# Layer 1's attention on ScalarE, VectorE and GpSimd: an order written by queues and slots in place of the scheduler's

## The chip, the core and the metric

The kernel runs on one core of one Trainium2 chip. The metric is the device time of one execution in microseconds (us). A core has five engines with instruction queues of their own: TensorE (PE, matmuls; PEld is its weight load), VectorE (DVE), ScalarE (ACT), GpSimd (POOL) and SyncE (SP, which issues the DMAs). An engine takes its instructions in the order in which they stand in its queue; an instruction that waits holds up all that stand behind it.

## What is computed

The reference is an encoder of two layers over 1024 tokens of width 1024, in fp32. Layer 0 mixes tokens with a neighbourhood attention, layer 1 with a dense differential attention of 8 heads; both end with a gated convolutional feed-forward part and a gated embedding. The change is in layer 1's attention:

```python
def diff_attention(h, w_qkv, lam, subln_g, w_o, t5_table, lambda_init):
    q, k, v = jnp.split(h @ w_qkv, 3, axis=-1)      # q, k: 8 heads x 2 maps of 64; v: 8 heads of 128
    ...
    def block_fn(args):                             # one block of 128 queries
        bias = t5_table[t5_bucket(kpos[None, :] - qpos[:, None])]
        s = jnp.einsum('bhmqd,bhmkd->bhmqk', qb, k).astype(jnp.float32) + bias[None, :, None]
        a = jax.nn.softmax(s, axis=-1)
        w = a[:, :, 0] - lam_full * a[:, :, 1]
        return jnp.einsum('bhqk,bhkd->bhqd', w.astype(v.dtype), v)
    o = lax.map(block_fn, (q_blocks, jnp.arange(nb)))
    ...
    o = rms_norm(o, subln_g) * (1.0 - lambda_init)
    return o @ w_o
```

## The kernel before

For fp32 accuracy on TensorE, each operand of a large matmul is split into a high part (ACT rounds it, `high`, L231) and a low part (DVE subtracts, `low`, L234); with a scale they are L241 and L242. One product of two such operands is three matmuls (L268, L269, L270).

Layer 1's attention (`da`) goes through 64 chunks: 8 heads by 8 blocks of 128 queries. The loop over n is software-pipelined and written in the order that PE follows word for word: `da_values(n-1)` (16 matmuls, L971), `da_scores(n+1)` (12 matmuls, L928), the first `da_turn(n)` (four transposes of the weights E, L955, which ACT copies into wT, L958), some of the stream, the second turn (copied at L960), some of the stream, `da_out(n-1)` (a transpose of the normed row os, L988, copied by ACT into ot at L996), and again the stream. Beside PE a chunk has on DVE: ss (L975), os (L980), two biased scores with their minimum (L750), then c, the sums' reciprocals (L938 to L940) and the weights E (L941); on POOL the root of ss (L280); on ACT the square (L974), the two exponentials (L754), wT twice, and ot.

The stream, `da_stream`, is a generator that makes the projections q, k and v and hands PE three matmuls for each unit; `tick` draws 6.3 units a chunk for the first 16 chunks and 5.3 after. The first two heads are projected plainly (`keys`, `queries`, `values`). All others come in nine `Pair`s, each two blocks of weights done by seven products instead of eight:

```python
PRODUCTS = (
    ("A11", "B11", 0), ("S2", "T2", 1), ("A12", "B21", 0), ("S3", "T3", 1), ("S1", "T1", 2), ("A22", "T4", 1), ("S4", "B22", 2),
)
```

Each names a weight operand (A or a sum S), an activation operand (B or a sum T) and one of three accumulators, which lie in two banks of PSUM by turns. So a product brings: a weight split (ws, ACT then DVE), S sums on POOL (L116 to L119), and an evacuation of a bank in `put`: p1 (ACT, L164), u (DVE, L166), c11 (ACT, L169, in v pairs), w (DVE, L173), c5 (ACT, L175), p2 (DVE, L181), u2 (DVE, L184), and w plus c5 on POOL (L178). For kq pairs the outputs are split into the head's q and k (L231 to L242); for v pairs PE turns them (L299, copied by ACT at L625; the plain ones from raw, L634). The T sums, 36 adds on POOL (L576 to L586), are made once at the start, split, sent to DRAM (L562) and loaded again for each pair (L595). Near the end the stream makes splits of the layer's input embeddings (L1892).

On PE the order is written out by hand; on ACT, DVE and POOL the tile framework's scheduler sets it, from a simulated timeline, with a few hints: `behind` and `job` put an instruction of the stream behind one of the attention, and `hurry` runs what is in a list of postponed splits, `jobs`.

Of the kernel before, what the change touches and what calls it, by code (L numbers as in the profile page):

```python
# [16 lines left out]
P = 128  # L17
# [81 lines left out]
class Pair:  # L99


    def __init__(self, trunk, W, room, kind, j):
        self.trunk, self.room, self.kind, self.j = trunk, room, kind, j
        self.src = (W[KT + j], W[j]) if kind == "kq" else (W[2 * KT + j], W[2 * KT + j + 1])
        self.A, self.o, self.ps, self.made, self.w = {}, {}, {}, [], 0
    def load(self, n):
        k = self.trunk
        w = k.page(k.raw, "raw", (P, KT, P))
        k.nc.sync.dma_start(w, self.src[n])
        self.A[f"A{n + 1}1"], self.A[f"A{n + 1}2"] = w[:, :4], w[:, 4:]  # L110

    def sums(self):
        A, tt = self.A, self.trunk.nc.gpsimd.tensor_tensor
        S = lambda n: self.room[:, n].rearrange("p (k n) -> p k n", k=4)
        A["S1"], A["S2"], A["S3"], A["S4"] = (S(n) for n in range(4))
        tt(out=A["S1"], in0=A["A21"], in1=A["A22"], op=ALU.add)  # L116
        tt(out=A["S2"], in0=A["S1"], in1=A["A11"], op=ALU.subtract)
        tt(out=A["S3"], in0=A["A11"], in1=A["A21"], op=ALU.subtract)
        tt(out=A["S4"], in0=A["A12"], in1=A["S2"], op=ALU.subtract)  # L119

    def operand(self, q):
        k, trunk = PRODUCTS[q][0], self.trunk

        def do():
            self.o[k] = trunk.operand(self.A[k])
            return trunk.did

        trunk.jobs.append(do)
# [8 lines left out]
    def bank(self, n, q):  # L137
        first = n not in self.ps
        if first:
            self.ps[n] = self.trunk.bank(self.trunk.pj)  # L140
        return self.ps[n], first

    def out(self, row, half, src, turns, turn, wait):

        k, j = self.trunk, self.j
        if self.kind == "v":
            turns.append([wait, turn(self.h[row], half, src, 2 * (j + row) + half)])
            return
        s = slice(half * 512, half * 512 + 512)
        if row:  # L150
            k.split(src, self.h[:, 0, s], self.h[:, 1, s], -0.125)
        else:
            k.split(src, self.h[:, 2, s], self.h[:, 3, s])
        self.made.append(src)
        if len(self.made) == 4:
            k.qk[j] = self.h

    def put(self, a, turns, turn):

        nc, ps = self.trunk.nc, self.ps  # L160
        tt, act = nc.vector.tensor_tensor, nc.scalar.activation
        c11, p1, u, w, c5 = (self.room[:, n] for n in (1, 4, 5, 6, 7))
        if a == "A11":
            act(p1, ps[0], AF.Copy)  # L164
        elif a == "S2":
            tt(out=u, in0=ps[1], in1=p1, op=ALU.add)  # L166
        elif a == "A12":
            if self.kind == "v":
                act(c11, ps[0], AF.Copy)  # L169
            self.out(0, 0, c11 if self.kind == "v" else ps[0], turns, turn, 2)  # L170
        elif a in ("S3", "S1"):
            if a == "S3":
                tt(out=w, in0=ps[1], in1=p1, op=ALU.add)  # L173
            else:
                act(c5, ps[2], AF.Copy)  # L175
            self.w += 1
            if self.w == 2:
                nc.gpsimd.tensor_tensor(out=w, in0=w, in1=c5, op=ALU.add)  # L178
                self.out(1, 1, w, turns, turn, 4)
        elif a == "A22":  # L180
            tt(out=p1, in0=ps[1], in1=p1, op=ALU.add)  # L181
            self.out(1, 0, p1, turns, turn, 3)
        else:
            tt(out=u, in0=ps[2], in1=u, op=ALU.add)  # L184
            self.out(0, 1, u, turns, turn, 3)


class Trunk:
# [328 lines left out]

    def da_stream(self, hT, x, first, mid):
# [4 lines left out]
        turns = []  # L523
        self.third = True

        def step():
            for t in turns:
                t[0] -= 1
            if self.open and turns and turns[0][0] < 0:
                turns.pop(0)[1]()  # L530
# [3 lines left out]
        def plain(w, tb, wait=None):  # L534
            s = slice(tb * 512, tb * 512 + 512)
            ps = self.bank(self.pj)
# [11 lines left out]
        tt, pool = nc.vector.tensor_tensor, nc.gpsimd.tensor_tensor  # L548
# [9 lines left out]
        made = []  # L558

        def put(m, key, t):  # L560
            did = self.split(t, ring[:, m % 4, 0], ring[:, m % 4, 1])
            nc.sync.dma_start(stash[key][m // 3], raw[:, m % 4])  # L562
            return did

        def sums(n):

            k = n // 2
            self.all_jobs()
            if made:
                self.jobs += [lambda a=a: put(*a) for a in made.pop()]  # L570
            if n == 8:
                return
            b = [tuple(f(a)[:, k] for a in x) for x in (B11, B12, B21, B22)]
            t1, t2, t3, t4 = room[:, k], room[:, 4 + 3 * (k % 2)], room[:, 5], room[:, 6]
            if n % 2 == 0:
                pool(out=t1, in0=b[1][0], in1=b[0][0], op=sub)  # L576
                pool(out=t1, in0=t1, in1=b[1][1], op=add)
                pool(out=t1, in0=t1, in1=b[0][1], op=sub)
                pool(out=t2, in0=b[3][0], in1=t1, op=sub)
                pool(out=t2, in0=t2, in1=b[3][1], op=add)  # L580
                made.append([(3 * k, "T2", t2)])
# [1524 lines left out]
```

## Time and profile before

| | |
|---|---|
| median of 3 executions | 2718.63 us (2714.75 to 2719.02) |
| profiled execution | 2721.1 us |
| its span | 2719.3 us (36972 instructions) |
| PE busy | 2665.1 us, 98% |
| DVE busy | 1970.9 us, 72% |
| ACT busy | 1373.0 us, 50% |
| POOL busy | 561.5 us, 21% |

The profile is one execution, taken by the hardware profiler. The profiled execution's own time is 1.8 us above its span. A row of the timeline reads: start us, duration us, engine, line, operation, output from inputs, form, count, and in brackets the idle time just before with what ended it. The layer-1 attention lies between about 1300 and 1910 us of the span.

### The profile page before, as it was taken

The page shows a single profiled execution, that of the slowest core. Times are in us where ns is not written, and L with a number is a line of the kernel's source. Part 1 is how long each engine was busy: PE and PEld are TensorE (multiplying, and loading weights), DVE is VectorE, ACT ScalarE, POOL GpSimd, SP SyncE. Part 2 cuts the span into 40 slices and gives each one's busy share as a digit, 9 for nine tenths or more (in the row PEclk, how much of TensorE's full clock was granted, in tenths as well). Part 3 has the DMA queues.
Part 4 walks back from the last instruction along what each step waited for, and adds up shares of the span by engine and source line. Part 5 has one row for each costly group of instructions (what it writes and reads, how often), then busy time and mean ns, then how long its engine had stood idle before and what let it go on. Part 6 is the DMA issues. An engine that isn't in the chain of part 4 may idle for free.

```text
span 2719.3 us, 36972 instructions
## 1 busy us (share of the span) xinstructions
PE 2665.1 (98%) x13384; PEld 2197.9 (81%) x13384; DVE 1970.9 (72%) x3379; ACT 1373.0 (50%) x2595; POOL 561.5 (21%) x526
## 2 busy tenths in 40 slices
PE   8999999999999999999999999999999999999999
PEld 6888887878888888888777877777878888878887
DVE  5777776699777777676667767776699777768674
ACT  5555556454444444554456666665454444444452
POOL 2221220003433300000722222210103334300000
PEclk9999999999999999999999999999999999999999
DMA  6223226424232373333345655552423333374342
GB/s 182 85 66 105 75 93 200 132 68 137 92 116 96 122 271 124 113 128 119 119 144 198 201 170 194 176 176 84 159 71 130 103 109 100 112 249 139 116 136 101
DMA packets 149785, 360.91 MB, mean 133 GB/s; under 512 B 14009, under 2 KB 40889, under 8 KB 149602
## 3 DMA queue, kind: packets, MB, share of 16 engines
q1 hardware_dynamic: 149602, 358.55, 40.3%
q8 instruction: 105, 1.72, 0.3%
q14 instruction: 78, 0.64, 0.1%
HBM read 277.79 MB, written 92.90 MB: 136 GB/s over the span
## 4 chain that ended last, share of the span: by engine, by line
PE 82%; DVE 7%; ACT 5%; issue 2%; POOL 2%; DMA 1%; SPq 0%; ACTq 0%; DVEq 0%; POOLq 0%
PE b L268 19%; PE b L269 19%; PE b L270 19%; PE g L1135 6%; PE m L1135 5%; PE b L971 3%; ACT E L754 2%; PE s L928 2%; PE b L299 2%; PE b L1135 2%; PE av L821 2%; PE b L955 1%; PE b L794 1%; DVE E L750 1%; DVE r L234 1%
## 5 line engine op out<-in xcount | busy, mean ns | idle before, releaser
L268 PE MATMUL b<-r,ws 128*128 128x512 f32 (+1 forms) x1308 | 533.2, 408 | 1.7 <-DVE r L403 1.7
L269 PE MATMUL b<-r,ws 128*128 128x512 f32 (+1 forms) x1308 | 506.3, 387 | 0.6 <-DVE r L234 0.5
L270 PE MATMUL b<-r,ws 128*128 128x512 f32 (+1 forms) x1308 | 506.7, 387 | 0.0
L754 ACT ACTIVATE E<-E,mn 128x1024 f32<-128x1024 f32 (+2 forms) x256 | 221.5, 866 | 148.3 <-DVE mn L750 148.1
L270 PEld LDWEIGHTS b<-r,ws 128*128 128x128 f32 x1308 | 246.8, 189 | 51.8
L268 PEld LDWEIGHTS b<-r,ws 128*128 128x128 f32 x1308 | 247.8, 189 | 47.6 <-issue 3.3
L269 PEld LDWEIGHTS b<-r,ws 128*128 128x128 f32 x1308 | 248.3, 190 | 35.6 <-DVE r L234 1.9
L268 PE MATMUL b<-r,wa 128*128 128x512 f32 x688 | 268.1, 390 | 1.9 <-DVE B L1527 1.9
L270 PE MATMUL b<-r,wa 128*128 128x512 f32 x688 | 267.9, 389 | 0.0
L269 PE MATMUL b<-r,wa 128*128 128x512 f32 x688 | 267.7, 389 | 0.0
L280 POOL TENSOR_TENSOR ss<-ss,mhalf 128x1 f32<-128x1 f32 x128 | 83.6, 654 | 857.7 <-DVE ss L276 382.1
L268 PE MATMUL b<-r,r 128*128 128x512 f32 x648 | 254.4, 393 | 1.3 <-DVE facc L1731 0.7
L269 PE MATMUL b<-r,r 128*128 128x512 f32 x648 | 252.8, 390 | 1.9 <-DVE r L234 1.9
L270 PE MATMUL b<-r,r 128*128 128x512 f32 x648 | 252.5, 390 | 0.0
L231 ACT ACTIVATE r<-raw 128x512 fp32r<-128x512 f32 (+1 forms) x168 | 108.7, 655 | 195.4 <-PE b L269 169.9
L234 DVE TENSOR_TENSOR ws<-raw,ws 128x512 fp32r<-128x512 f32 (+3 forms) x177 | 170.8, 971 | 49.6 <-ACT ws L231 48.0
L231 ACT ACTIVATE ws<-raw 128x512 fp32r<-128x512 f32 (+3 forms) x177 | 122.3, 697 | 109.0 <-PE b L270 52.0
L234 DVE TENSOR_TENSOR r<-raw,r 128x512 fp32r<-128x512 f32 (+1 forms) x168 | 124.8, 749 | 70.3 <-ACT r L231 67.3
L1135 PE MATMUL m<-r,ws 128*128 128x512 f32 x672 | 157.3, 392 | 0.0
L1135 PE MATMUL g<-r,ws 128*128 128x512 f32 x672 | 155.8, 391 | 0.0
L268 PEld LDWEIGHTS b<-r,wa 128*128 128x128 f32 x688 | 129.1, 188 | 29.9 <-DVE B L1527 3.2
L750 DVE CUSTOM_DVE_ANT_0 E<-s,T 128x1024 f32<-128x1024 f32 x128 | 151.1, 1216 | 1.0 <-PE s L928 0.9
(227 smaller groups left out, 5344.9 us busy)
## 6 DMA issues: line engine op xcount, KB each, us to landing
r<-stashT SPq DMA_DIRECT2D x108, 512.0 KB, 4.5
raw<-in_w_in SPq DMA_DIRECT2D x86, 512.0 KB, 3.5
raw<-in_qkv SPq DMA_DIRECT2D x48, 512.0 KB, 3.9
spillS<-r SPq DMA_DIRECT2D x88, 256.0 KB, 2.7
r<-in_ffn_w_out SPq DMA_DIRECT2D x40, 512.0 KB, 6.6
raw<-spillS SPq DMA_DIRECT2D x40, 512.0 KB, 3.6
spillA<-B SPq DMA_DIRECT2D x66, 256.0 KB, 2.7
raw<-spillA SPq DMA_DIRECT2D x30, 512.0 KB, 3.9
```

What stands on the lines that cost most here:

```text
L231: return self.nc.scalar.activation(hi, src, AF.Copy).ins
L234: return self.nc.vector.tensor_tensor(out=lo, in0=src, in1=hi.bitcast(F32), op=ALU.subtract).ins
L268: mm(out, sta[0], mov[0], start=first, stop=False, skip_group_check=onto)
L269: mm(out, sta[0], mov[1], start=False, stop=False, skip_group_check=onto)
L270: mm(out, sta[1], mov[0], start=False, stop=last, skip_group_check=onto)
L280: self.nc.gpsimd.tensor_tensor(out=ss, in0=ss, in1=self.mhalf, op=ALU.pow)
L299: self.nc.tensor.transpose(t[:, k * P : k * P + P], h[:, c : c + P], self.ident)
L750: nc.vector.tensor_tensor_reduce(out=e, in0=s, in1=bias, scale=1.0, scalar=3e38, op0=ALU.add, op1=ALU.min, accum_out=mn)
L754: self.exp = nc.scalar.activation(e, e, AF.Exp, bias=mn, scale=-1.0, accum_out=sm).ins
L821: nc.tensor.matmul(out, V[:, kb, m], a[:, at : at + w].rearrange("p k t -> p (k t)"), start=g % 2 == 0 and i + z == 0, stop=g % 2 == 1 and ...
L971: nc.tensor.matmul(o, wT[:, k], V[:, k], start=k == 0, stop=k == KT - 1)
L1135: mm(out[half], a, b[:, w], start=first and k + z == 0, stop=last and k == n - 1 and z == 2)
```

## The change

The attention of layer 1 gets a region in which ACT, DVE and POOL follow the program's order as PE does; it begins before `da_scores(0)` and ends at the last product:

```python
+            self.region = self.tc.manual_schedule(engines={ENG.Activation, ENG.DVE, ENG.Pool})
+            self.region.__enter__()
...
+            if last and q == 6:
+                self.flush()
+                self.third = False
+                self.region.__exit__(None, None, None)
```

What a product needs besides PE is no longer issued at once. Each split, sum and evacuation goes into a queue ("A" for ACT, "D" for DVE, "G" for POOL) with a modelled cost, a key, the keys that must come first, and a modelled date from which it is ready. `slot` takes from such a queue as long as room is left, evacuations first (`hot`) and weight splits after other things; `force` takes what PE is about to need, with what must come first:

```python
+    def later(self, eng, do, cost, key=None, first=(), ready=None):
+        self.queue[eng].append((do, cost, key, first, self.now if ready is None else ready))
+    def slot(self, eng, room, at, urgent=False):
+        q, end = self.queue[eng], at + room
+        self.now = at
+        while end - at > 0.3:
+            can = [
+                n for n, (_, _, _, first, ready) in enumerate(q)
+                if ready <= at and all(k in self.did_keys and self.ready_at.get(k, 0) <= at for k in first)
+            ]
+            hot = [n for n in can if q[n][2] and self.hot & set(q[n][2])]
+            if not (hot if urgent else can):
+                return
+            cold = [n for n in can if not (q[n][2] and q[n][2][0] == "a")]
+            at += self.pop(eng, (hot or cold or can)[0], at)
+    def force(self, *keys):
+        for key in keys:
+            while key not in self.did_keys:
+                ...
+                self.pop(eng, n)
```

The places in a chunk are fixed, by a modelled clock of 8.6 us for each chunk:

```python
             for n in range(N + 1):
+                self.now = self.base = 8.6 * n + self.extra
...                                               # da_values: behind the root, ahead of os
+            self.slot("A", 1.3, at + 2.5), self.slot("D", 0.7, at + 2.7), self.slot("G", 4.3, at + 3.3)
...
                     self.da_turn(x, n, 0)
+                if n + 1 < N:
+                    self.da_exp(n + 1, 0)
+                self.now = self.base + 3.9
                 self.tick(0.34)
                 if n < N:
                     self.da_turn(x, n, 1)
+                if n + 1 < N:
+                    if self.third:
+                        self.slot("A", 0.7, self.base + 6.7, True)
+                    self.da_exp(n + 1, 1)
+                    if self.third:
+                        self.slot("D", 1.6, self.base + 6.4)
+                    self.da_weights(n + 1)
...
                     self.da_out(x, n - 1, oT)
+                if self.third:
+                    self.slot("G", 2.8, self.base + 7.8), self.slot("A", 1.9, self.base + 8.4), self.slot("D", 1.2, self.base + 10.1)
```

For this the softmax is cut in three: `biased` (both biased scores in `da_scores`), `da_exp` and `da_weights`. Smaller parts: the T sums are planned for units 10, 17, 24, ... 59 instead of 10, 18, 27, ... 76; a pair's second load and its S sums come one product earlier (at products 2 and 4 instead of 3 and 5); kq pairs copy c11 out on ACT too, as v pairs did, instead of splitting it from the bank (six more ACT copies); turns of v wait until their source is ready by the model; a head's q and k are handed over when its splits are asked for; the embeddings' first two loads come together and their splits go through the queues:

```python
-        plan = {u: lambda n=n: sums(n) for n, u in enumerate((10, 18, 27, 36, 45, 53, 61, 68, 76))}
-        plan |= {58: lambda: pairs[0].load(0), 70: lambda: pairs[0].load(1), 80: first_operands, 83: first_sums}
+        plan = {u: lambda n=n: sums(n) for n, u in enumerate((10, 17, 24, 31, 38, 45, 52, 59))}
+        plan |= {60: lambda: pairs[0].load(0), 70: lambda: pairs[0].load(1), 76: late_stash, 80: first_operands, 83: first_sums}
...
-            if self.kind == "v":
-                act(c11, ps[0], AF.Copy)
-            self.out(0, 0, c11 if self.kind == "v" else ps[0], turns, turn, 2)
+            k.later("A", lambda: act(c11, ps[0], AF.Copy), 0.6, key("c11"), mine("S2"))
+            self.out(0, 0, c11, turn)
+            k.holds(ps[0], key("c11"))
...
-            if after and q == 3:
-                self.all_jobs()
+            if after and q == 2:
                 after.load(1)
-            if after and q == 5:
-                self.all_jobs()
+            if after and q == 4:
                 after.sums()
```

PE's and SP's instructions stay the same in number; a few turns of v and the embeddings' units shift by some units of the stream. What moves on ACT and DVE is shown at three places. Names: E the (biased, then exponentiated) scores, mn and sum their minimum and sum, b a bank of PSUM, r pages of split operands or of the products' room, ws split weights.

ACT at the start of the attention, before: the exponentials of chunk 0 (L754), with the table load, then a T split, a copy of v (L634), a weight split, two T splits and the first wT copy.

```order
L241 ACTIVATE r_1548_11126<-b_1559_11238 128x512
L754 ACT_TABLE_LOAD
L754 ACTIVATE E_1566_11292,sum_11296<-E_1566_11292,mn_11294 128x1024
L754 ACTIVATE E_1567_11293,sum_11300<-E_1567_11293,mn_11298 128x1024
L231 ACTIVATE r_1549_11127<-r_1550_11128 128x512
L634 ACTIVATE raw_11270<-b_1562_11271 128x512
L231 ACTIVATE ws_11339<-raw_11337 128x1024
L231 ACTIVATE r_1549_11127<-r_1550_11128 128x512 x2
L958 ACTIVATE wT_11401<-b_1587_11402 128x512
```

The same place now (L249 is the high part, L598 a scaled or plain high part of q or k, L1110 the exponential, L1136 the wT copy):

```order
L249 ACTIVATE r_1549_11127<-r_1550_11128 128x512
L598 ACTIVATE r_1548_11126<-b_1560_11239 128x512
L249 ACTIVATE r_1549_11127<-r_1550_11128 128x512 x3
L772 ACTIVATE raw_11281<-b_1563_11282 128x512
L249 ACTIVATE ws_11342<-raw_11237 128x1024
L1110 ACT_TABLE_LOAD
L1110 ACTIVATE E_1567_11313,sum_11319<-E_1567_11313,mn_11315 128x1024
L1110 ACTIVATE E_1568_11314,sum_11320<-E_1568_11314,mn_11317 128x1024
L1136 ACTIVATE wT_11391<-b_1586_11392 128x512
```

Four T splits, the copy of v and the weight split moved ahead of the table load and the first exponential.

ACT in chunk 28, before, from the square (L974) to ot (L996):

```order
L974 ACTIVATE os_14069,ss_14070<-b_2125_14060,sum_13929 128x128
L231 ACTIVATE ws_14074<-raw_13617 128x512
L958 ACTIVATE wT_14108<-b_2139_14109 128x512
L754 ACTIVATE E_2131_14092,sum_14096<-E_2131_14092,mn_14094 128x1024
L169 ACTIVATE r_1550_11128<-b_2088_13889 128x512
L960 ACTIVATE wT_14108<-b_2141_14125 128x512
L754 ACTIVATE E_2132_14093,sum_14100<-E_2132_14093,mn_14098 128x1024
L231 ACTIVATE ws_14131<-r_1550_11128 128x512
L996 ACTIVATE ot_14139<-b_2125_14060,subg 128x128
```

Now, from the square (L1150) to ot (L1172) and the split behind it:

```order
L1150 ACTIVATE os_14082,ss_14083<-b_2127_14073,sum_13936 128x128
L1136 ACTIVATE wT_14111<-b_2139_14112 128x512
L1110 ACTIVATE E_2132_14102,sum_14109<-E_2132_14102,mn_14104 128x1024
L1136 ACTIVATE wT_14111<-b_2140_14127 128x512
L184 ACTIVATE r_1550_11128<-b_2088_13891 128x512
L1110 ACTIVATE E_2133_14103,sum_14110<-E_2133_14103,mn_14106 128x1024
L1172 ACTIVATE ot_14145<-b_2127_14073,subg 128x128
L249 ACTIVATE ws_14148<-r_1550_11128 128x512
```

The copy of c11 out of bank b_2088 moved from between the first exponential and the second wT copy to behind that copy, and the weight split from ahead of the first wT copy away to behind ot.

DVE in chunk 41, before, from the first biased score (L750) to the weights (L941); L181 is p2, L242 a low part:

```order
L750 ISA E_2357_15176,mn_15178<-s_15162,T_11275 128x1024
L750 ISA mn_15178 128x1
L750 ISA E_2358_15177,mn_15182<-s_15163,T_11275 128x1024
L750 ISA mn_15182 128x1
L181 TENSOR_TENSOR r_1550_11128<-b_2311_14942,r_1550_11128 128x512
L938 RECIPROCAL c_15186<-sum_15184 128x1
L234 TENSOR_TENSOR ws_15219<-r_1550_11128,ws_15219 128x512
L939 SCALAR_TENSOR_TENSOR c_15186<-sum_15180,c_15186,neglam 128x1
L242 SCALAR_TENSOR_TENSOR r_2293_14869<-r_1550_11128,r_2293_14869 128x512
L940 RECIPROCAL sum_15180<-sum_15180 128x1
L941 SCALAR_TENSOR_TENSOR E_2357_15176<-E_2358_15177,c_15186,E_2357_15176 128x1024
```

Now, from behind the weights of the chunk before (L188 is p2, L252 a low part, L1151 ss, L1156 os, L1103 the biased scores) to the last reciprocal, behind which the weights L1120 stand:

```order
L188 TENSOR_TENSOR r_1550_11128<-b_2310_14940,r_1550_11128 128x512
L252 TENSOR_TENSOR ws_15143<-r_1550_11128,ws_15143 128x512
L1151 TENSOR_SCALAR ss_15168<-ss_15168 128x1
L252 TENSOR_TENSOR ws_15145<-raw_14938,ws_15145 128x512
L1156 TENSOR_SCALAR os_15167<-b_2352_15158,sum_15021,ss_15168 128x128
L1103 ISA E_2357_15190,mn_15192<-s_15176,T_11296 128x1024
L1103 ISA mn_15192 128x1
L1103 ISA E_2358_15191,mn_15194<-s_15177,T_11296 128x1024
L1103 ISA mn_15194 128x1
L1117 RECIPROCAL c_15222<-sum_15197 128x1
L1118 SCALAR_TENSOR_TENSOR c_15222<-sum_15196,c_15222,neglam 128x1
L1119 RECIPROCAL sum_15196<-sum_15196 128x1
```

p2 and a low part moved from between the biased scores and the weights to ahead of ss, and nothing stands between the reciprocals any more.

More of the change, by code (lines that the diff above doesn't have):

```diff
@@ L115, in sums @@
[L115 to L119, printed above, removed]
-    def operand(self, q):
[L122 to L128, printed above, removed]
+        A, k, prev = self.A, self.trunk, self.prev
@@ L130, in begin, with high @@
+    def operand(self, q):
+        a, k = PRODUCTS[q][0], self.trunk
+        def high():
+            o = self.o[a] = k.page(k.ws, "ws", (P, 2, 4, P), F32R)
+            k.high(self.A[a], o[:, 0])
+            k.later("D", lambda: k.low(self.A[a], o[:, 0], o[:, 1]), 0.75, self.key(a), ready=k.ends + 0.1)
+        k.later("A", high, 0.62, self.key(a + " high"), [self.key(a + " sum")] if a[0] == "S" else [], self.loaded)
     def begin(self, x):
@@ L516, in qkv_stream, with pop @@
             yield from self.second_out()
+    def later(self, eng, do, cost, key=None, first=(), ready=None):
+        self.queue[eng].append((do, cost, key, first, self.now if ready is None else ready))
+    def pop(self, eng, n=0, at=None):
+        do, cost, key, first, ready = self.queue[eng].pop(n)
+        self.force(*first)
+        self.ends = (self.now if at is None else at) + cost
+        if key is not None:
+            self.ready_at[key] = self.ends
+        do()
+        self.did_keys.add(key)
+        return cost
@@ new lines, in turn_now, with flush, split_later, high @@
+    def turn_now(self, key):
+        n = [t[2] for t in self.turns].index(key)
+        for t in self.turns[: n + 1]:
+            t[1]()
+        del self.turns[: n + 1]
+    def flush(self):
+        while any(self.queue.values()):
+            self.pop(next(e for e in "DAG" if self.queue[e]))
+    def split_later(self, src, hi, lo, scale=None, key=None, cost=(0.62, 0.75), first=(), ready=None):
+        nc = self.nc
+        def high():
+            if scale is None:
+                self.high(src, hi)
+            else:
+                nc.scalar.activation(hi, src, AF.Copy, scale=scale)
+            self.later("D", low, cost[1], key, ready=self.ends + 0.1)
+        def low():
+            if scale is None:
+                self.low(src, hi, lo)
+            else:
+                nc.vector.scalar_tensor_tensor(out=lo, in0=src, scalar=scale, in1=hi.bitcast(F32), op0=ALU.mult, op1=ALU.subtract)
+        self.later("A", high, cost[0], key and (*key, "high"), first, ready)
@@ L518, in da_stream, with take, holds @@
+    def take(self):
+        if len(self.banks) == 2:
+            self.force(*self.banks.pop(0)[1])
+        ps = self.bank(self.pj)
+        self.banks.append((ps, []))
+        return ps
+    def holds(self, ps, key):
+        next(b for b in self.banks if b[0] is ps)[1].append(key)
     def da_stream(self, hT, x, first, mid):
@@ L1866, in embeddings @@
         todo = [lambda n=n: job(n) for n in range(4)]
-        self.jobs += todo[:2]
+        if x is None:
+            self.jobs += todo[:2]
+        else:
+            begin(self.raw, "raw"), begin(self.raw, "raw")
+            for n in range(2):
+                self.split_later(raws[n], *a[n], None, ("a", n), (1.05, 1.25))
         self.after_values = [] if layer else todo[2:]
```

325 lines of the change are left out of this document (209 added, 116 removed).

## Prediction

> **What bounds the kernel now.** I read the page first: how busy the engines are and which of them carries the chain that ended last.
>
> ```profile
> span 2719.3 us, 36972 instructions
> PE 2665.1 (98%) x13384; PEld 2197.9 (81%) x13384; DVE 1970.9 (72%) x3379; ACT 1373.0 (50%) x2595; POOL 561.5 (21%) x526
> PE 82%; DVE 7%; ACT 5%; issue 2%; POOL 2%; DMA 1%; SPq 0%; ACTq 0%; DVEq 0%; POOLq 0%
> ```
>
> PE is 98% busy and carries 82% of the chain. The change leaves PE's instructions as they are, so it can win only PE's idle time and the time in which PE is throttled, and only where attention of layer 1 runs, 1310 to 1910 us. So the second view is the busy time of each engine in four stretches of it, and, for the clock, one short window (the columns are: window, its length, busy us of PE, PEld, DVE, ACT, POOL with their counts, granted clock, DMA share, GB/s).
>
> ```profile
> 1310.00:1340.00 30.00, 26.38 (x148) 20.25 (x144) 21.80 (x25) 14.62 (x25) 29.21 (x20) 1.00 0.30 107
> 1340.00:1400.00 60.00, 54.10 (x327) 43.41 (x328) 42.17 (x80) 34.82 (x73) 20.24 (x19) 0.97 0.37 130
> 1400.00:1800.00 400.00, 390.57 (x2483) 315.74 (x2482) 288.19 (x572) 250.86 (x528) 92.04 (x86) 1.00 0.57 192
> 1800.00:1910.00 110.00, 102.50 (x619) 83.20 (x618) 72.71 (x143) 65.10 (x135) 6.57 (x12) 0.97 0.29 98
> ...
> 1392.00:1394.00 2.00, 2.00 (x7) 1.51 (x6) 1.72 (x5) 1.44 (x5) 0.00 (x0) 0.50 0.97 347
> ```
>
> PE's idle time is 3.6, 5.9, 9.4 and 7.5 us, together 26.4 us. The clock of 0.97 in two stretches is a loss of its own: 3% of 60 us is 1.8 us and of 110 us 3.3 us, together 5.1 us. It falls to 0.50 behind a wait, as the last row shows. **At most 26.4 + 5.1 = 31.5 us, 1.2%, can be won.** Third, the waits of PE there (engine, line, what it waited for: total us, times, longest):
>
> ```profile
> PE b L988 <- DVE os L980: 8.2, 5, 3.5
> PE b L971 <- ACT wT L960: 4.0, 7, 1.0
> PE b L299 <- ACT wT L960: 2.5, 2, 1.7
> PE b L268 <- ACT ws L1892: 2.5, 2, 1.8
> PE b L299 <- ACT wT L958: 1.9, 1, 1.9
> PE b L955 <- DVE ss L975: 1.6, 2, 1.3
> PE b L299 <- ACT raw L634: 1.3, 1, 1.3
> ...
> PEld b L971 <- ACT wT L960: 8.9, 12, 1.4
> ```
>
> Nearly all name a softmax result that came late (os, wT), and the late ones have sums or splits in front of them. One steady chunk, last, for the durations:
>
> ```profile
> 1508.03 1.95 PE L971 MATMUL b<-v,wT 128*128 128x128 f32 x16
> 1511.35 0.68 DVE L234 TENSOR_TENSOR ws<-r,ws 128x512 fp32r<-128x512 f32 x1
> 1512.47 0.41 DVE L980 TENSOR_SCALAR os<-b,sum,ss 128x128 f32<-128x128 f32 x1 [0.44 <-POOL ss L280]
> 1512.80 1.21 DVE L750 CUSTOM_DVE_ANT_0 E<-s,T 128x1024 f32<-128x1024 f32 x1
> 1515.20 0.58 ACT L960 ACTIVATE wT<-b 128x512 f32<-128x512 f32 x1
> 1515.68 1.14 ACT L754 ACTIVATE E<-E,mn 128x1024 f32<-128x1024 f32 x1
> 1516.01 1.95 PE L971 MATMUL b<-v,wT 128*128 128x128 f32 x16
> 1517.48 1.27 DVE L941 SCALAR_TENSOR_TENSOR E<-E,c,E 128x1024 f32<-128x1024 f32 x1
> ```
>
> From values to values (L971) the chunk takes 1516.01 − 1508.03 = 7.98 us, and it waits nowhere. DVE and ACT are 72% and 63% busy between 1400 and 1800 (288.19 and 250.86 of 400): there is room in sum, so only order matters.
>
> **The gains.** (1) The longest os wait:
>
> ```profile
> 1383.46 2.99 DVE L234 TENSOR_TENSOR r<-r,r 128x512 fp32r<-128x512 f32 x3
> 1387.56 1.00 POOL L280 TENSOR_TENSOR ss<-ss,mhalf 128x1 f32<-128x1 f32 x1
> 1390.82 0.33 PE L988 MATMUL b<-ident,os 128*128 128x128 f32 x1 [3.50 <-DVE os L980]
> 1809.85 0.33 PE L988 MATMUL b<-ident,os 128*128 128x128 f32 x1 [2.60 <-DVE os L980]
> ```
>
> Three low parts stand on DVE ahead of ss, POOL takes the root late, and os falls behind both biases. With the written order os stands before the biases in every chunk, with at most one filler between ss and it. I count the 3.5 us as won, and 1.0 of the three short ones (8.2 − 3.5 − 2.6 = 2.1), and the half clock behind it: 1.8 us. The 2.6 us at 1809.85 stays: four splits of the embeddings stand there in the new order too. Sum 6.3.
>
> (2) The waits for the second wT copy, 4.0 + 2.5 us. Before, an evacuation could stand between the first exponential and that copy; the order now has 4 such fillers in the whole attention for 13. Won in proportion, 9/13 of 6.5 = 4.5. Of PEld's 8.9 us, 4.9 more than PE's own, I count a third, 1.5. The raw wait of 1.3 and the ss wait of 1.3 go too, since raw copies now wait for a modelled date and no split stands inside the weights chain (15 before, none now): 2.6. Sum 8.6.
>
> **The costs.** (3) The start of attention:
>
> ```profile
> 1313.32 2.54 POOL L579 TENSOR_TENSOR r<-r,r 128x512 f32<-128x512 f32 x2
> 1309.63 1.28 ACT L754 ACT_TABLE_LOAD   x1
> 1312.54 1.15 ACT L754 ACTIVATE E<-E,mn 128x1024 f32<-128x1024 f32 x1 [1.64 <-DVE mn L750]
> 1315.99 2.20 DVE L941 SCALAR_TENSOR_TENSOR E<-E,c,E 128x1024 f32<-128x1024 f32 x1
> 1318.15 1.05 ACT L231 ACTIVATE ws<-raw 128x1024 fp32r<-128x1024 f32 x1
> 1321.16 0.66 PE L955 MATMUL b<-ident,E 128*128 128x128 f32 x4
> 1324.56 0.63 ACT L231 ACTIVATE r<-r 128x512 fp32r<-128x512 f32 x1 [5.36 <-POOL r L584]
> 1326.96 0.66 PE L299 MATMUL b<-ident,raw 128*128 128x128 f32 x4 [1.93 <-ACT wT L958]
> ```
>
> ACT's queue is now written: four T splits, a raw copy, a weight split and the table load stand ahead of the first exponential, and the last of these splits needs POOL's 14th T sum. Before, the 14th ended at 1313.32 + 2.54 = 1315.86, when the exponentials were over. From there: two splits 1.26, raw copy 0.58 (as wT's), weight split 1.05, table 1.28, to 1320.0; two exponentials at 1.25 with their read-outs, to 1322.5; c and weights 3.2 as before (from 1312.54 + 2 × 1.25 = 1315.0 to the end of L941, 1318.19, with POOL adding beside them) or, with L941 at 1.27 and POOL idle, about 1.7: to 1324.2 or 1325.7. PE wanted the turn at 1321.16: it waits 3.0 to 4.5 us, I take 3.6, about the middle. It replaces the 1.9 at 1326.96, and I add 1.8 for half clock behind it, since the wait of 3.50 had it and the one of 1.93, where the granted clock stayed 1.00, had not. Net 3.6 − 1.9 + 1.8 = 3.5.
>
> [...]
>
> (4) Evacuations in fixed places. A copy from PE's bank that stood ahead of exponentials now stands behind the second wT copy or later; an ACT copy takes 0.58 us, and where PE's next product wants the bank in the same chunk (chunks 14, 20, 29, 41, 50) the product waits. In five chunks, 0.6 us each (one ACT copy): 3.0. No wait for a bank shows before; so the bounds are 0 (the copy has the other bank's product as cover) and 5 × 1.14 = 5.7 (an exponential ahead of each); a gain is excluded, because no wait is there to win. In a written order a filler that waits for its own input also holds up all that is queued behind it: on ACT the next exponential, on DVE the next bias, on POOL the next root. The fillers are dealt by a model of 8.6 us for each chunk, where this one takes 7.98, so an input can be up to 0.6 us later than dealt; I put that into the range, not into the sum.
>
> (5) Splits of the embeddings, 4 × 0.63 = 2.5 us, stand on ACT between the first exponential and the second wT copy of a chunk near the end: 1.0 (0 if the stream ahead of that chunk's values covers them, 2.5 if nothing does; I take a value nearer 0, because the fourth of a chunk's stream that follows the second turn lies there, some 0.16 × 8 = 1.3 us). First operand of the first pair, whose low now follows both biases: 0.5 (0 to 1.2). A u2 sum that now stands behind L941 while the last turn of the first v pair wants it: 1.0 (0 to 1.27). Sum 2.5.
>
> The six more c11 copies, 6 × 0.58 = 3.5 us on ACT, cost nothing while ACT is 63% busy; if that cover goes they cost 3.5. Pair loads issued one product earlier, on SP, and the T sums, planned closer together on POOL, cost nothing but what (3) has: no wait of PE names a load in this stretch, and POOL is 92.04 of 400 us busy after 1400.
>
> **Sum:** −6.3 − 8.6 + 3.5 + 3.0 + 2.5 = −5.9 us against the profiled execution, 2719.3 + 1.8 around the span = 2721.1, hence 2715. That execution lies 2.5 us above the median of the runs, 2718.63, so the forecast in the runs' terms is 2718.6 − 5.9 = 2712.7; of the 4.4 us of idle time that the quoted waits do not name (26.4 − 22.0) I count a third, 1.5, as won, thus **2711**. For no change I take ±0.2%, 5.4 us, about what a measurement of this kernel can tell: the gain is just above it, and the likeliest case's own range is 2703 to 2716.
>
> **The rivals.** (A) Slower: the place of evacuations becomes PE's wait. There are 63 products, each with one. Before, they went when ready. If each bank comes 0.3 us late in mean, the cost (4) is 63 × 0.3 = 19 us instead of 3: −14.9 + 3.5 + 2.5 + 19 = +10, 2729. It decides from (14.9 − 6.0 + 5.4)/63 = 0.23 us in mean, above which the kernel is slower by over 0.2%. For it: both biases are 2 × 1.21 us during which DVE takes nothing else, and an ACT copy can meet 1.14. Against: a product is 12 matmuls and banks are two, so most have a product's time to spare. Chance 0.22.
>
> (B) Nothing measurable: the gains are real, but the start costs 4.5 + 1.8, DVE's fillers between L941 and ss (71 now, 51 before) make new os waits of 0.7 us (one low part) in 10 chunks: −5.9 + 0.9 + 7 = +2.0, which is 2721, or with half of the new os waits 2718. Chance 0.22.
>
> (C) Nearly all waits go: of 31.5 us remain the 3.6 + 1.8 at the start and the embeddings' 2.6; 2718.6 − 31.5 + 8 = 2695. For it: DVE and ACT have room in sum, and a chunk without fillers in its way waits nowhere. Against: the start alone keeps 5.4. Chance 0.15.
>
> (D) POOL holds DVE. L941 took 1.27 us alone and 2.20 us beside POOL's sums at 1315.99, and POOL now has five T sums in a row (5 × 1.27 = 6.4 us) in each of four early chunks, so that a root behind them also waits: 4 to 6 chunks by 0.93 us is 5 us, and the result 2716. Against: the T sums end early in attention. Chance 0.08. [...]
>
> **How the numbers follow.** The own forecast has 0.33, A 0.22, B 0.22, C 0.15, D 0.08. Faster by over 0.2% is below 2713.2: all of C, 0.15, three quarters of the own forecast, 0.25, and a third to a half of B and D by their low ends, 0.12; together 0.52. Slower by over 0.2% is above 2724: nearly all of A, 0.20, and B's high end, 0.02. The rest, 0.26, is within. The range runs from C less 3 us (one embedding wait gone as well), 2692, to A, 2729; below it I leave 0.06 and above it, where banks come over 0.3 us late, 0.11.
>
> **What would show it.** (1) right if no wait for os of over 1.5 us is left near 1390, and the clock of 0.50 there is gone. (2) right if the waits for the second wT copy come to under 2 us. (3) right if PE's first turn of E waits 3 to 4.5 us for the weights. (4) shows as waits of L268 on the copies of p1, c11 and c5, or on u, p2; over 15 us of them is rival A. D shows as L941 at over 2 us. The idle time of PE from 1310 to 1910 should be near 21 us for 26.4, of which 8 in the first 30 us. The forecast would be wrong if PE's order hid a wait at products that no row of before has.

## The result, and the profile after

The changed kernel takes 2697.95 us (median of 4, 2696.8 to 2699.0) for 2716.69 us before (median of 4, 2714.09 to 2719.02): a ratio of 0.9931, 95% interval 0.9914 to 0.9948. It is faster by 0.7%, some 19 us, where 2711 was forecast: the sign and the range held, the likeliest case's own range, 2703 to 2716, did not. Its profiled execution took 2696.8 us. The two profiled executions lie 24.3 us apart (2721.1 and 2696.8), more than the medians, at mean granted clocks of 0.997 and 0.999; of 13 further executions of the kernel before, the three at 0.999 took 2715.6 to 2715.9 us and the six at 0.997 took 2717.4 to 2720.7.

The busy times by stretch show where the time came from (columns as in the prediction; the attention is the same work, though it ends some 23 us earlier here, so the last window reaches further into what follows):

```profile
span 2695.0 us, 36988 instructions
PE 85%; DVE 6%; ACT 3%; issue 2%; DMA 2%; POOL 1%; SPq 0%; DVEq 0%; ACTq 0%; POOLq 0%
...
1310.00:1340.00 30.00, 26.77 (x140) 21.58 (x141) 16.75 (x28) 15.08 (x26) 12.77 (x10) 0.94 0.34 123
1340.00:1400.00 60.00, 58.79 (x368) 47.56 (x368) 49.95 (x84) 38.20 (x82) 32.90 (x27) 1.00 0.40 139
1400.00:1800.00 400.00, 396.24 (x2536) 322.61 (x2533) 299.31 (x593) 263.12 (x550) 81.08 (x88) 1.00 0.57 195
1800.00:1910.00 110.00, 107.08 (x631) 87.36 (x630) 75.48 (x139) 62.56 (x131) 8.77 (x16) 1.00 0.36 118
```

PE is idle for 11.1 us of these 600, for 26.4 before. Of the half clock, 5.1 us before, 1.8 us (6% of 30) are left, all in the first window. The waits of PE in 1310 to 1910 us are now these, 10.4 us in all for 25.8 (L1133 is the turn of E, L286 to L288 the three matmuls of a product, L759 the copy of a turned v, L2092 the copy of the embeddings' products, L1892 before):

```profile
PE b L1133 <- DVE E L1120: 4.0, 2, 3.2
PE b L1164 <- DVE os L1156: 2.3, 2, 1.3
PE b L286 <- ACT ws L2092: 1.4, 2, 0.7
PE b L1147 <- ACT v L759: 0.8, 1, 0.8
PE b L1147 <- ACT wT L1136: 0.7, 1, 0.7
PE b L1331 <- ACT ws L2092: 0.5, 1, 0.5
PE b L286 <- DVE r L194: 0.5, 1, 0.5
PE b L288 <- DVE ws L252: 0.2, 1, 0.2
```

Read against the list of before: L1164 is the transpose of os, 2.3 us for 8.2; L1147 is values, and L317 (turns of v), which waited 5.7 us for wT and raw, is gone. 3.2 us of the first row are the start that term (3) of the prediction described. The rows of L286 for r and of L288 are all that the evacuations and operands in fixed places cost: 0.7 us. The embeddings' copies (ws L2092) cost 1.9 us for 4.1; of before, the list in the prediction has 2.5 of these, and this row the rest:

```profile
PE b L1135 <- ACT ws L1892: 1.6, 1, 1.6
```

### The profile page after: what moved, and what is told of

The parts are those of the page before. It is cut to its first block, busy times and chain, and to the rows that moved or that the text cites. A ratio compares the mean times of both kernels' runs of the same rounds, so it can differ in the third digit from the quotient of the medians.

```text
span 2695.0 us, 36988 instructions
## 1 busy us (share of the span) xinstructions
PE 2658.3 (99%) x13384; PEld 2195.6 (81%) x13384; DVE 1971.6 (73%) x3380; ACT 1377.5 (51%) x2600; POOL 547.9 (20%) x526
## 4 chain that ended last, share of the span: by engine, by line
PE 85%; DVE 6%; ACT 3%; issue 2%; DMA 2%; POOL 1%; SPq 0%; DVEq 0%; ACTq 0%; POOLq 0%
PE b L286 19%; PE b L287 19%; PE b L288 19%; PE g L1331 6%; PE m L1331 5%; PE b L1147 4%; PE s L1092 3%; PE b L1133 2%; PE b L317 2%; PE b L1331 2%; PE av L985 2%; PE b L958 1%; ACT E L1110 1%; DVE r L252 1%; DMA x<-in_x 1%
## 5 line engine op out<-in xcount | busy, mean ns | idle before, releaser
L286 PE MATMUL b<-r,ws 128*128 128x512 f32 (+1 forms) x1308 | 533.2, 408 | 2.4 <-DVE r L421 1.7
L288 PE MATMUL b<-r,ws 128*128 128x512 f32 (+1 forms) x1308 | 506.5, 387 | 0.2 <-DVE ws L252 0.2
L288 PEld LDWEIGHTS b<-r,ws 128*128 128x128 f32 x1308 | 246.4, 188 | 52.6 <-DVE ws L252 1.0
L286 PEld LDWEIGHTS b<-r,ws 128*128 128x128 f32 x1308 | 247.1, 189 | 50.7 <-issue 3.3
L298 POOL TENSOR_TENSOR ss<-ss,mhalf 128x1 f32<-128x1 f32 x128 | 76.0, 595 | 959.6 <-DVE ss L1151 430.6
L286 PE MATMUL b<-r,wa 128*128 128x512 f32 x688 | 268.0, 390 | 2.0 <-DVE B L1723 2.0
L288 PE MATMUL b<-r,wa 128*128 128x512 f32 x688 | 267.9, 389 | 0.0
L286 PE MATMUL b<-r,r 128*128 128x512 f32 x648 | 254.4, 393 | 1.2 <-DVE facc L1927 0.6
L288 PE MATMUL b<-r,r 128*128 128x512 f32 x648 | 252.4, 390 | 0.0
L249 ACT ACTIVATE r<-raw 128x512 fp32r<-128x512 f32 (+1 forms) x168 | 108.7, 655 | 194.3 <-PE b L287 169.1
L252 DVE TENSOR_TENSOR ws<-raw,ws 128x512 fp32r<-128x512 f32 (+3 forms) x177 | 171.2, 973 | 44.8 <-ACT ws L249 42.5
L249 ACT ACTIVATE ws<-raw 128x512 fp32r<-128x512 f32 (+3 forms) x177 | 122.4, 698 | 108.1 <-PE b L288 51.9
L252 DVE TENSOR_TENSOR r<-raw,r 128x512 fp32r<-128x512 f32 (+1 forms) x168 | 124.7, 748 | 71.2 <-ACT r L249 68.2
L1110 ACT ACTIVATE E<-E,mn 128x1024 f32<-128x1024 f32 x128 | 146.8, 1147 | 20.1 <-DVE mn L1103 18.1
L286 PEld LDWEIGHTS b<-r,wa 128*128 128x128 f32 x688 | 129.1, 188 | 29.9 <-DVE B L1723 3.3
L288 PEld LDWEIGHTS b<-r,wa 128*128 128x128 f32 x688 | 129.1, 188 | 27.9 <-DVE wa L252 1.1
```

Of the source, the lines that this page charges most:

```text
L249: return self.nc.scalar.activation(hi, src, AF.Copy).ins
L252: return self.nc.vector.tensor_tensor(out=lo, in0=src, in1=hi.bitcast(F32), op=ALU.subtract).ins
L286: mm(out, sta[0], mov[0], start=first, stop=False, skip_group_check=onto)
L288: mm(out, sta[1], mov[0], start=False, stop=last, skip_group_check=onto)
L298: self.nc.gpsimd.tensor_tensor(out=ss, in0=ss, in1=self.mhalf, op=ALU.pow)
L1110: self.exp = self.nc.scalar.activation(e, e, AF.Exp, bias=mn, scale=-1.0, accum_out=sm).ins
```

## The experiments

### Is it the order that gains, or what the program says?

Two kernels separate the two. The first keeps the new program and takes the written order away, by a region that names PE alone:

```diff
-            self.region = self.tc.manual_schedule(engines={ENG.Activation, ENG.DVE, ENG.Pool})
+            self.region = self.tc.manual_schedule(engines={ENG.PE})
```

> The changed kernel without its region: queues, slots, cut softmax, earlier T sums and the rest stay, but ACT, DVE and POOL are placed by the scheduler again. Theory T (the gain is the fixed order on ACT, DVE and POOL, which keeps fillers from between ss and os, and from ahead of the second wT copy): most of the gain of 18.7 us is lost, 2710 to 2720, and waits for os and wT are back at 8 us or more. Rival R1 (the program's new sequence and dates are enough, whoever places them): within 3 us of the changed kernel, 2695 to 2702.

Measured: 2718.02 us, ratio to before 1.0004 (0.9994 to 1.0013). All of the gain is gone, as theory T says. PE's waits in 1310 to 1910 us:

```profile
PE b L1164 <- DVE os L1156: 6.9, 6, 2.6
PE b L317 <- ACT wT L1136: 5.3, 5, 2.4
PE b L1147 <- ACT wT L1136: 4.2, 6, 1.5
PE b L1147 <- ACT v L759: 2.8, 2, 2.3
```

os waits 6.9 us for 8.2 before, wT 9.9 us (with a row of 0.4 that is not shown) for 8.4: the waits are back, that of os a little below the 8 us expected. The second puts the cut softmax into the kernel before (`da_exp` behind each turn, `da_weights` behind the second):

```diff
...
+                if n + 1 < N:
+                    self.da_exp(n + 1, 0)
                 self.tick(0.34)
...
+                if n + 1 < N:
+                    self.da_exp(n + 1, 1)
+                    self.da_weights(n + 1)
```

> The kernel before with one part of the change alone: the softmax cut in three, so that in the program each exponential follows a turn and the weights follow the second exponential; the scheduler places it. Theory T: no gain of more than 4 us, 2713 to 2720, since the scheduler sets the order anyway. Rival R1: half of the gain or more, 2708 or less.

Measured: 2716.42 us, ratio 0.9996 (0.9987 to 1.0005). Nothing, so R1 falls twice.

### Which engine's order?

Three kernels leave one engine each to the scheduler and keep the other two in the written order; only the set in `manual_schedule` differs.

> The changed kernel with ACT and POOL in the written order and DVE left to the scheduler. Theory D1 (os and the biases were late because of what stood on DVE): most of the gain goes, 2709 or more, with os waits of over 5 us. Rival D2 (ACT's order carries the gain): 2702 or less.

> The changed kernel with DVE and POOL in the written order and ACT left to the scheduler. Theory D1: 2698 to 2704, a few waits for wT come back. Rival D2: 2709 or more, with waits for wT of 8 us or more.

> The changed kernel with ACT and DVE in the written order and POOL left to the scheduler. Theory D3 (the root behind POOL's sums made the longest os wait, with the order of POOL alone): the os wait and half clock come back between 1380 and 1400 us, 2703 or more. Theories D1 and D2: POOL has room after 1400 us, 2697 to 2701.

| written order on | time, us | ratio to before | above the changed kernel |
|---|---|---|---|
| all three | 2697.95 | 0.9931 (0.9914 to 0.9948) | |
| ACT, POOL | 2705.31 | 0.9961 (0.9946 to 0.9976) | 7.4 |
| DVE, POOL | 2699.57 | 0.9940 (0.9924 to 0.9957) | 1.6 |
| ACT, DVE | 2711.16 | 0.9980 (0.9970 to 0.9989) | 13.2 |
| none | 2718.02 | 1.0004 (0.9994 to 1.0013) | 20.1 |

POOL, the engine that is busy least, costs most when its order is left out. Not all of its 13.2 us is lost in steady chunks: at the start ACT waits longer for POOL's sums (7.5 us at a time for 4.7), PE waits 4.9 us for the first turn instead of 3.2, and the half clock lasts 6.8 us instead of 3.4, from 1322.8 us, still in the wait, to 1329.6 by windows of 1 us (clock 0.57 over 1322 to 1330; PE works in 4.3 us of it, so 2.1 us are lost for 1.7). DVE's share lies between D1's and D2's numbers, without the long os waits that D1 expected (1.5 us in all). D1's number for ACT (2698 to 2704) held; ACT's share seems small, but without its order the scheduler puts the first exponentials earlier and wins the start (1310 to 1340: PE busy 29.61 us at clock 1.00), so what it loses behind that is more than 1.6 us. D3 has the size right and the place wrong: no long wait for os came back near 1390 (the half clock near there follows a wait of 1.9 us for wT, at 1401 us). The shares are what is lost when one order is left out; they need not add up to the whole.

```profile
PE b L1133 <- DVE E L1120: 4.9, 1, 4.9
```

What DVE waits for, over the attention, shows the mechanism. Before, without POOL's order, and changed, one row each:

```profile
DVE os L980 <- POOL ss L280: 27.8, 38, 3.0
```

```profile
DVE os L1156 <- POOL ss L298: 46.9, 50, 2.9
```

```profile
DVE os L1156 <- POOL ss L298: 30.0, 45, 0.7
```

os waits for the root in 38 to 50 of the 64 chunks; in the written order never over 0.7 us, the root itself (0.55 us) and its way. Left to the scheduler, a sum can stand ahead of the root. One such place in the kernel without POOL's order:

```profile
1543.85 1.28 POOL L129 TENSOR_TENSOR r<-raw 128x512 f32<-128x512 f32 x1 [3.37 <-DVE ss L1151]
1545.08 0.55 POOL L298 TENSOR_TENSOR ss<-ss,mhalf 128x1 f32<-128x1 f32 x1
...
1545.67 0.41 DVE L1156 TENSOR_SCALAR os<-b,sum,ss 128x128 f32<-128x128 f32 x1 [1.83 <-POOL ss L298]
1546.00 1.21 DVE L1103 CUSTOM_DVE_ANT_0 E<-s,T 128x1024 f32<-128x1024 f32 x1
...
1547.25 1.15 ACT L1110 ACTIVATE E<-E,mn 128x1024 f32<-128x1024 f32 x1 [1.91 <-DVE mn L1103]
...
1549.02 0.50 PE L286 MATMUL b<-r,ws 128*128 128x512 f32 x1 [1.04 <-DVE r L182]
```

A sum of 1.28 us goes ahead of the root; os waits 1.83, both biases stand behind os on DVE, the first exponential waits 1.91 for the first of them, and the evacuation behind the biases (r L182) keeps PE waiting 1.04. So one POOL sum in the wrong place delays three engines.

### Is it the dates of the T sums?

```diff
-        plan = {u: lambda n=n: sums(n) for n, u in enumerate((10, 17, 24, 31, 38, 45, 52, 59))}
+        plan = {u: lambda n=n: sums(n) for n, u in enumerate((10, 18, 27, 36, 45, 53, 61, 68))}
...
-            if after and q == 2:
+            if after and q == 3:
                 after.load(1)
-            if after and q == 4:
+            if after and q == 5:
                 after.sums()
```

> The changed kernel with the old dates: T sums at units 10, 18, 27, 36, 45, 53, 61, 68, second pair load and S sums one product later. Theory T: 2695 to 2702, and no os wait of over 1.5 us, for the fixed place of os ahead of the biases keeps it whatever the dates are. Rival R2 (the 3.5 us wait for os and its half clock went because the T sums were made earlier): a wait of 2 us or more comes back between 1380 and 1400 us and the time is 2702 to 2705. At the start the old dates put fewer T sums ahead of the first exponential (9 for 14), so both also expect the wait for the first turn to shrink by up to 3 us.

Measured: 2701.88 us, ratio 0.9940 (0.9925 to 0.9955). By the medians 3.9 us, by the ratios 2.4 us of the gain are the dates' and the earlier loads'. The time lies at the edge of theory T's range, just below R2's, and T's sign holds: os waits 1.2 us at most. The loss is a wait of 1.8 us of L317 for wT, over at 1398 us, with half clock behind it, and 1.4 us for a weight split's low part. The wait for the first turn shrank by 1.0 us only, to 2.2, and has no half clock behind it (1.00 in 1310 to 1340).

### The start

```diff
             self.da_scores(x, 0)
+            self.da_exp(0, 0), self.da_exp(0, 1)
             self.tick(12 / 6)
+            self.da_weights(0)
             self.extra = self.now
...
-            self.da_exp(0, 0), self.da_exp(0, 1)
-            self.da_weights(0)
```

The first kernel has this and the third group of T sums at unit 26 for 24:

> The changed kernel with the start eased: the third group of T sums two units later, and the first two exponentials written right behind the first scores, ahead of the copy of v and the weight split. Theory (the wait of 3.2 us for the first turn and the half clock behind it, 1.8 us, come from what stands ahead of these exponentials on ACT): both go, 4 to 5 us, 2693 to 2694. Rival (the T sums and splits put off there make os or wT late in the next chunks): 2 us or less is won, 2696 or more, with new waits between 1325 and 1400 us.

Measured: 2697.3 us, ratio 0.9922 (0.9906 to 0.9939): hardly anything. Both sides of the expectation were half right. The first stretch has PE 29.96 us busy at clock 1.00, so the start's 5 us are won; the next loses them (waits of 1.9 us for wT, 1.4 for a low part and 1.3 for E, with half clock):

```profile
1310.00:1340.00 30.00, 29.96 (x174) 24.25 (x174) 17.55 (x30) 17.62 (x32) 8.64 (x8) 1.00 0.26 92
1340.00:1400.00 60.00, 55.17 (x332) 44.24 (x329) 49.31 (x81) 35.47 (x73) 35.98 (x30) 0.97 0.42 146
```

The second leaves the dates alone:

> The changed kernel with only the first two exponentials written right behind the first scores; the T sums keep their new dates. Theory S (the wait of 3.2 us for the first turn and its half clock come from ACT's order alone; the eased start gave its 5 us back because there the T sums were late): 4 to 5 us faster than the changed kernel, 2693 to 2694, and no waits of 1.3 us and more at 1344, 1377 and 1392 us. Rival (whatever takes the wait at the start away only moves it, since DVE and POOL are then the bound of the first chunks): 2696 to 2698, with such waits.

Measured: 2693.35 us (2692.75 to 2694.08), ratio 0.9911 (0.9896 to 0.9925), 4.6 us less than the changed kernel. The first exponentials stand at 1313.90 and 1315.71 us, the first turn waits for nothing, and nothing comes back:

```profile
1313.90 1.16 ACT L1110 ACTIVATE E<-E,mn 128x1024 f32<-128x1024 f32 x1 [1.47 <-DVE mn L1103]
...
1315.71 1.14 ACT L1110 ACTIVATE E<-E,mn 128x1024 f32<-128x1024 f32 x1
...
1310.00:1340.00 30.00, 29.62 (x170) 23.74 (x166) 21.06 (x32) 18.07 (x32) 15.92 (x13) 1.00 0.34 125
1340.00:1400.00 60.00, 58.86 (x369) 47.15 (x367) 49.92 (x86) 38.37 (x79) 30.80 (x26) 1.00 0.40 138
```

So term (3) was the place of these exponentials in ACT's order. This edit also moves the first weights on DVE; but the kernel with only ACT left to the scheduler, in which these weights keep their place, has the start free too. Two units of delay of one group of T sums cost about 4 us, nearly what the start did.

### Evacuations: earlier, and later

The urgent place ahead of the second turn, and so of the second wT copy:

```diff
+                if self.third:
+                    self.slot("A", 0.7, self.base + 6.7, True)
+                    self.now = self.base + 3.9
                 if n < N:
                     self.da_turn(x, n, 1)
                 if n + 1 < N:
-                    if self.third:
-                        self.slot("A", 0.7, self.base + 6.7, True)
```

> The changed kernel with the urgent place for evacuations on ACT moved from behind the second wT copy to ahead of it, where the scheduler often had them. Theory T (an evacuation ahead of that copy delays PE's values): some nine evacuations of 0.58 us move there, so 2 to 4 us of waits of L1147 or L317 for wT come back, 2699 to 2702. Rival A in small (banks are what PE waits for): the few waits of L286 go and the time falls by 1 us, 2697.

Measured: 2694.69 us (2694.22 to 2698.16), ratio 0.9918 (0.9903 to 0.9933). Nine evacuations stand there now, none in the changed kernel, and PE's values wait 0.7 us for wT as before them. Theory T was wrong in this point: in the written order these evacuations ahead of the copy do not delay PE. Why the median is 3.3 us lower stays open: two chunks, 37 and 40 counted from 0, became 0.34 and 0.38 us shorter and one 0.27 longer, the waits named in the profile are 10.6 us for 10.4, and the intervals of the two ratios overlap.

Without the urgent place:

```diff
-                    if self.third:
-                        self.slot("A", 0.7, self.base + 6.7, True)
```

(In two pairs POOL then forms S4 before S2, because a late c11 of the pair before holds S2 back. S4 is so made from what lies in S2's place at that time, and this kernel no longer computes the reference; number and kind of the instructions stay, and only its times are used.)

> The changed kernel without the urgent place: an evacuation on ACT waits for the place behind ot, unless a product that must have its bank calls it. Rival A (fixed places make PE wait for banks): each evacuation that was urgent is now some 2 to 3 us later, and PE waits in L286 for p1, c11 or c5, 5 us or more in all, 2703 or more. Theory T with cover (a bank is written again only a product, 2.7 us, or more later, and the places behind ot come in time): 2697 to 2700.

Measured: 2705.78 us, ratio 0.9957 (0.9940 to 0.9974). Rival A's mechanism, at the place where it was looked for:

```profile
PE b L286 <- ACT r L190: 2.9, 2, 1.8
PE b L286 <- ACT r L184: 2.8, 3, 1.1
...
PE b L286 <- ACT r L180: 1.4, 1, 1.4
```

PE waits 7.1 us for c5, c11 and p1, six times. With the urgent place none of these rows is there.

### The embeddings

```diff
-        self.jobs += todo[:2]
+        if x is None:
+            self.jobs += todo[:2]
+        else:
+            begin(self.raw, "raw"), begin(self.raw, "raw")
+            self.jobs += [lambda n=n: self.split(raws[n], *a[n]) for n in range(2)]
...
-            while len(done) < 2:
+            while self.jobs:
                 self.hurry()
...
-            done += [2, 3]
+            done += range(4)
```

> The kernel before with the change's embeddings alone: both first loads at once. Between the works that stood at 1800 and 1873 us before, the kernel without the region gained 4.6 us of its profile and the one with the softmax cut alone gained nothing there. Theory E (the embeddings' earlier loads did that): 4 to 5 us gained in that stretch, 2712 to 2713, and the second half clock, at 1842 us, gone. Rival (it was the queue, which has all sums and splits of the last pair done before the embeddings' splits): no change, 2715 to 2719.

Measured: 2717.4 us, ratio 0.9999 (0.9989 to 1.0008): theory E falls. Its profile is 3 us shorter in that stretch all the same, at the same waits, because the half clock at 1811 us and the one at 1842 us are both missing. Of this kernel, then of the one before:

```profile
1809.57 0.33 PE L988 MATMUL b<-ident,os 128*128 128x128 f32 x1 [2.60 <-DVE os L980]
...
1811.00:1815.00 4.00, 4.00 (x33) 3.45 (x31) 2.45 (x6) 1.65 (x5) 0.41 (x1) 1.00 0.07 23
```

```profile
1811.00:1815.00 4.00, 4.00 (x18) 3.57 (x17) 2.33 (x5) 1.47 (x5) 0.00 (x0) 0.57 0.13 45
```

os waits 2.60 us in both, and only one has the half clock behind it; the second place, at 1842 us before, is alike (waits of 1.84 and 1.85 us, clock 0.57 and 1.00). That the rival's queue shortened the embeddings' waits was not tried.

### Both edits together

> Both edits that helped: the first two exponentials right behind the first scores, and the urgent evacuations ahead of the second wT copy. If their gains are apart (4.6 us at the start, 0.7 us of chunks 37 to 56 in the profile), 2692 to 2693 and 11 to 12 us less idle and throttled time of PE than with neither would not be reached: about 5 us less. If they meet, no faster than 2693.4.

Measured: 2691.86 us (2691.55 to 2692.84), ratio 0.9913 (0.9899 to 0.9928); the fastest median of all, and at the low end of what was expected if the two gains are apart. From the kernel with the exponentials alone its ratio cannot be told apart. In the profile the attention is about 1 us shorter than there. Left, in 600 us: 7.9 us of idle PE (600 − 592.07), no half clock.

## Why the prediction was right in sign and short in size

By the named waits of PE in 1310 to 1910 us and the half clock (sum −18.8, for a forecast of −7.4; the profile's attention is 22 us shorter, the rest in short stalls that no wait names). That the sum agrees with the 18.7 us between the medians is chance: it is a sum over the two profiled executions, which lie 24.3 us apart.

| term | forecast | measured | from |
|---|---|---|---|
| (1) os and its half clock | −6.3 | −11.0 | os 8.2 to 2.3; three old stretches of half clock, 5.1, gone, of which 3.4 not shown to be the order's |
| (2) wT, raw, ss, E, v, ot | −8.6 − 1.5 | −10.0 | 11.6 to 1.6, without the start and the 0.7 of (5) |
| (3) start | +3.5 | +3.0 | wait 3.2 for 1.9, half clock 1.7 |
| (4) banks | +3.0 | +0.5 | L286 for L194; none for p1, c11, c5 |
| (5) embeddings' splits, first operand, u2 | +2.5 | +0.9 | 0.7 for wT behind the splits, 0.2 for a low part; u2 is in (4) |
| embeddings' copies (ws L1892) | 0 | −2.2 | 4.1 to 1.9 |

- **(1) had its waits nearly right; what it missed is half clock.** The waits for os fell by 5.9 us (4.5 forecast), and 1.7 us of half clock behind the longest went (1.8 forecast). The two other stretches, at 1811 and 1842 us, I had left standing. They are gone too, 3.4 us, but the kernel with the embeddings' loads alone has neither of them behind the same two waits; so that part can be chance of the profiled execution. Of what I named (low parts ahead of ss, a late root, os behind both biases) the low parts alone do not make PE wait. In the changed kernel four stand there, and PE does not wait:

```profile
1388.86 2.49 DVE L252 TENSOR_TENSOR r<-r,r 128x512 fp32r<-128x512 f32 x4
1391.27 0.15 DVE L1151 TENSOR_SCALAR ss<-ss 128x1 f32<-128x1 f32 x1
1391.49 0.55 POOL L298 TENSOR_TENSOR ss<-ss,mhalf 128x1 f32<-128x1 f32 x1 [8.86 <-DVE ss L1151]
1392.08 0.41 DVE L1156 TENSOR_SCALAR os<-b,sum,ss 128x128 f32<-128x128 f32 x1 [0.66 <-POOL ss L298]
1392.40 1.22 DVE L1103 CUSTOM_DVE_ANT_0 E<-s,T 128x1024 f32<-128x1024 f32 x1
...
1394.35 0.27 PE L1164 MATMUL b<-ident,os 128*128 128x128 f32 x1
```

  The root finds POOL free, and os goes ahead of the biases, with 1.9 us to spare (1394.35 − 1392.49). Before, the root stood behind a sum of POOL, and os behind both biases:

```profile
1385.87 1.74 POOL L118 TENSOR_TENSOR r<-raw,raw 128x512 f32<-128x512 f32 x1
...
1388.08 1.21 DVE L750 CUSTOM_DVE_ANT_0 E<-s,T 128x1024 f32<-128x1024 f32 x1
...
1390.36 0.40 DVE L980 TENSOR_SCALAR os<-b,sum,ss 128x128 f32<-128x128 f32 x1
```

  And the wait of 2.6 us at the end, which I kept, fell to 1.3 by the row of waits.
- **(2) had its size right and its reason only in part.** I put PE's waits for the second wT copy down to evacuations ahead of it. Before, 13 stood there, but only three of the nine waits had one in front of them (0.96, 0.90 and 0.23 us). Ahead of all nine the first exponential had itself waited 1.2 to 4.0 us for the biased scores. One wait with both:

```profile
1644.27 1.16 ACT L754 ACTIVATE E<-E,mn 128x1024 f32<-128x1024 f32 x1 [1.96 <-DVE mn L750]
...
1645.42 0.57 ACT L231 ACTIVATE r<-b 128x512 fp32r<-128x512 f32 x1
...
1646.53 2.05 PE L971 MATMUL b<-v,wT 128*128 128x128 f32 x16 [0.90 <-ACT wT L960]
```

  Over the attention, ACT waited 63.4 us for the biased scores before, and now 18.1 us; with that, nine evacuations in the same place cost nothing (above). That the late exponential is the cause of each wait is read from these rows and was not tested by itself.

```profile
ACT E L754 <- DVE mn L750: 63.4, 56, 4.0
```

```profile
ACT E L1110 <- DVE mn L1103: 18.1, 28, 2.4
```

- **(3) was right**: E of the first turn was forecast 3.0 to 4.5 us late, and 3.2 us are measured, with the half clock. L941's successor takes 1.27 us there, with POOL idle by then.
- **(4) was the step that failed, and part of (5).** (4) put an ACT copy's full length on PE in five chunks where the order showed no slack. The bank's real slack I had not measured: no wait for p1, c11 or c5 came, and 0.5 us for u2, for 3.0 forecast. The experiment without the urgent place shows both: placed behind ot, six such copies do cost 7.1 us. In (5) the embeddings' splits cost 0.7 us for 1.0, as described:

```profile
1782.16 2.18 ACT L249 ACTIVATE r<-raw 128x512 fp32r<-128x512 f32 x4
...
1784.87 2.05 PE L1147 MATMUL b<-v,wT 128*128 128x128 f32 x16 [0.71 <-ACT wT L1136]
```

- **The embeddings' copies were put at nothing.** They wait 2.2 us less. The kernel without the written order has the same 1.9 us left, and the one with the earlier loads alone still 4.1: so neither the order nor these loads brought it, and what did is open.
- **Two numbers of the working** do not follow from its terms: half of B's new os waits gives 2717, not 2718, and the start's terms leave 3.6 − 1.9 + 3.6 = 5.3 us of idle PE in the first 30 us, not 8. Measured are 3.2 there and 11.1 in all, for 21.
- **The rivals.** A is real but not here. The long weights that D named came and their price did not: in four early chunks in a row, with POOL's T sums beside them, the weights took 2.3 us, and once PE waited 0.75 us for them; but before, five took 2.2 to 2.3 us as well, and the mean over the 64 chunks is 1345 ns for 1342. The result lies 3 us above C's price of 2695 and 13 below my forecast: with the start as forecast, nearly all other waits went, as C had it.

```profile
1370.50 2.33 DVE L1120 SCALAR_TENSOR_TENSOR E<-E,c,E 128x1024 f32<-128x1024 f32 x1
...
1372.98 0.63 PE L1133 MATMUL b<-ident,E 128*128 128x128 f32 x4 [0.75 <-DVE E L1120]
```

## What to carry to other kernels

An engine that is 20% busy can still cost the most when its order is left to the scheduler (POOL here, 13.2 us): look for short steps of a critical chain (here a root of 0.55 us) that queue behind its long ones, and write the order of all the engines of the chain together, since a written order on one hands on the lateness of another (behind one sum of 1.28 us os waited 1.83 us, an exponential 1.91 and PE 1.04). Price a moved instruction by the slack at its new place, measured in the trace, and not by its length; then test the price by moving it once earlier and once later. When a start or an edge looks late, move only what stands in front of it: the same edit with one group of T sums two units later lost about 4 of 5 us again.

## What the hardware showed that was not expected

- A stretch of half clock behind a wait of PE lasts about 3.4 us here and costs 1.7 us (before, three stretches cost 5.1 us), but which wait brings it is no matter of the wait's length alone: 2.60 us for os brought it in one kernel (0.57 over 1811 to 1815 us) and the same 2.60 us did not in another (1.00); a wait of 1.84 us had it (0.57 over 1842 to 1846 us), and one of 1.85 us had not (1.00 over 1838 to 1842 us). What decides was not shown.
- Without POOL's order the half clock at the first turn lasted twice as long, 6.8 us, and began while PE still waited (4.9 us in all): from 1323 to 1325 us PE is idle and the clock 0.50.
